# A two-layer hybrid backbone: layer 1's normalised input stored as two halves by the u projection and loaded as halves by the z projection

## The chip, the core and the metric

The kernel runs on one core of one Trainium2 chip. The time is the device time of one launch in microseconds (us). All data are 32-bit floats; a matmul operand is given as two parts, a rounded half ("hi") and the rest ("lo"), and each product is three matmuls: hi·hi, hi·lo and lo·hi.

## The reference, cut to what matters

Layer 0 is windowed attention, layer 1 a bidirectional state-space layer (S5). The change touches layer 1's input only:

```
h  = rmsnorm(x, norm_w[1]) * (1.0 + scale[:, None]) + shift[:, None]     # 2048 x 1024, called h1 here
u, z = jnp.split(h @ w_in, 2, axis=-1)                                   # w_in 1024 x 2048
...                                                                      # two scans over u, forward and backward
y  = gelu(y.reshape(b, l, SSM_WIDTH), approximate=False)
ya, yg = jnp.split(y @ w_glu, 2, axis=-1)
out = ((ya * sigmoid(yg)) * silu(z)) @ w_out
```

Both u and z are products of the same h1. The kernel computes u early and z much later, so h1 has to come a second time from somewhere.

## The kernel before, in words

Time runs through numbered phases: the attention layer (phases 1 and 2), the u projection (phase 3, about 1318 to 1520 us in the profile), the chunk states of the S5 layer (phase 4, to about 1696), the z projection with the scan over chunks (about 1696 to 1930), the S5 outputs (phase 5), and the GLU and output projection (phases 6 and 7). Tensor tiles are 128 partitions deep; "L1425" is line 1425 of the kernel.

**Order.** The code names an engine for each instruction; a scheduler that runs when the program is built sets the order of instructions on each engine, and a few instructions are pinned. Each engine works through its own row in that order. DMAs are issued from the row of SyncE ("SPq") or of ScalarE ("ACTq", through the helper `st`, L136), so a transfer whose buffer isn't free holds up all that stands behind it in the same row.

**u projection** (`phase3`, L1236). Eight blocks u of 256 tokens. `prep(u)` loads two row blocks of the layer's input x1d (L1255, tiles `qta` and `qtb` in turn, block 0 as `xt`), normalises them, and calls `prep3` (L1205) four times: TensorE transposes, ScalarE scales and shifts into an unrounded tile `hf` (named `kctx` in the profile, L1213), VectorE rounds it to `hi` (L108), VectorE or GpSimd subtracts to `lo` (L111). `st(store, hf)` then writes the unrounded tile, 256 KB, to the DRAM scratch `h1d` on ScalarE's queue: 32 such stores in all. TensorE multiplies the halves of block u while block u+1 is prepared.

**z projection** (`zproj`, L1427). The loops are nh (two halves of the 8 column blocks n) over u (8 token blocks) over np (two pairs of n): 16 passes (nh, u), called blocks i below. In each, 4 quarters q of the depth are multiplied for each n, 6 matmuls each: 96 a block, 1,536 in all. The weights of a column block n are loaded raw and split (`load_w`, tiles `wzh`, `wzl`; the low half on VectorE for n < 4, on GpSimd for n >= 4). `load_h` loads 256 KB of h1d into a raw tile `zraw` (4 buffers, shared with the weights, L1457), rounds it on ScalarE (L106), and subtracts on GpSimd (L111) into one of five tiles `zh0` to `zh4`; block 0 does some of this on VectorE. A block's four loads are asked for during the second pair of the block before. The result goes through ScalarE (`zo`, L1496, Silu) to the scratch z1d.

**The scan** (`scan`, L1405) runs on VectorE in the same stretch: 142 steps that each depend on the one before, a step being two multiplications (L1420) and four additions (L1425) with both inputs in SBUF, except the first two steps, whose products lie in PSUM (`kps`). Phase 5 (`rest`, first matmuls at L1669, their operand `xT` copied by ScalarE from the scan's result `sall`, L1662 and L1664) needs the finished scan. `first` and `early` (L1569, L1743) prepare tables for it: they are called inside the z projection's loop. Among them are L1536, L1539, L1544, L1561 and L1564 on VectorE and L1531, L1560 and L1592 on GpSimd.

Of the kernel before, what the change touches and what calls it, by code (L numbers as in the profile page):

```python
# [6 lines left out]
F32 = mybir.dt.float32  # L7
F32R = mybir.dt.float32r
# [9 lines left out]
KT = 8  # L18
# [47 lines left out]
ZH = ['vv', 'vv', 'vg', 'vv']  # L66
SZ = 2
# [18 lines left out]
class Net:  # L86
# [1118 lines left out]
    def prep3(self, k, src, t, hi, lo, r, store=None, hf=None):  # L1205
        nc = self.nc
        for kk in range(2):
            for j in range(2):
                nc.tensor.transpose(t[:, kk, j * 128:(j + 1) * 128], src(j, (k + kk) * 128), self.ident)
        if hf is None:  # L1210
            hf = self.k3()
        for kk in range(2):
            nc.scalar.activation(hf[:, kk], t[:, kk], AF.Identity, scale=self.g1[:, k + kk, r:r + 1],  # L1213
                                 bias=self.s1[:, k + kk, r:r + 1])
        self.split(hi[:, k:k + 2], lo[:, k:k + 2], hf, "v", "g" if k % 4 else "v")
        if store is not None:
            self.st(store, hf)

    def phase3_open(self):
        nc, a = self.nc, self.a  # L1220
# [15 lines left out]
    def phase3(self, uy):  # L1236
        nc, a = self.nc, self.a
        with ExitStack() as es:
# [12 lines left out]
            def prep(u):  # L1251
                if u:
                    xs = self.kp.tile([128, 2, D], F32, name=("qta", "qtb")[u % 2])
                    for j in range(2):
                        nc.sync.dma_start(xs[:, j], self.xrows(2 * u + j))  # L1255
                else:
                    xs = x0
                ss = sq.tile([128, 2], F32, name="ss3")
                for j in range(2):
                    junk = sq.tile([128, D], BF16, name="junk3", bufs=1)  # L1260
                    nc.scalar.activation(junk, xs[:, j], AF.Square, accum_out=ss[:, j:j + 1])
                r = self.rstd(sq, ss, 2)
                for j in range(2):
                    (nc.vector if u == 0 and j == 0 else nc.gpsimd).tensor_scalar(xs[:, j], xs[:, j], r[:, j:j + 1], 1.0, op0=OP.mult,
                                                                                  op1=OP.mult)
                hi = sm.tile([128, KT, 256], F32R, name="hi3")
                lo = sm.tile([128, KT, 256], F32R, name="lo3")
                for k in range(0, KT, 2):
                    self.prep3(k, lambda j, c: xs[:, j, c:c + 128], ps.tile([128, 2, 256], F32, name="tp3"), hi, lo, 0,
                               self.h1d[u][:, k:k + 2],  # L1270
                               xh.tile([128, 2, 256], F32, name=f"hf{k}") if u == 0 and k < 4 else None)
                H[u] = (hi, lo)

# [153 lines left out]
    def zproj(self, ps, first, early, scan):  # L1427
# [5 lines left out]
        pc = ec.enter_context(self.pool("zpc"))  # L1433

        def raw_tile():
            return pc.tile([128, 512], F32, name="zraw", bufs=4)

        W = {}

# [8 lines left out]
        H = {}  # L1448
        nh_ = [0]

        def load_h(u, qs, eng="g"):
            hs = H.setdefault(u, [])
            for q in qs:
                if nh == 0 and u == 0 and q == SZ:
                    next(scan)
                raw = raw_tile().rearrange("p (k c) -> p k c", k=2)
                nc.sync.dma_start(raw, self.h1d[u][:, q * 2:q * 2 + 2])  # L1457
                slot = nh_[0] % 5
                nh_[0] += 1
                h = (pc if slot == 4 else pa).tile([128, 2, 2, 256], F32R, name=f"zh{slot}")  # L1460
                self.split(h[:, 0], h[:, 1], raw, *(ZH[q] if eng == "v" else ("a", "g")))
                hs.append(h)

        if SZ < 0:
# [1 line left out]
        for nh in range(2):  # L1466
            for u in range(8):
                for np in range(2):
                    ns = [nh * 4 + np * 2, nh * 4 + np * 2 + 1]
                    if u == 0:  # L1470
                        load_w(ns[0])
                        if np == 0:
                            H.clear()
                            load_h(u, range(4), "v" if nh == 0 else "g")
                        load_w(ns[1])
                    ahead = np == 1 and u + 1 < 8
                    if ahead:
                        load_h(u + 1, (0,))
                    hs = H[u]
                    if (nh, u, np) == ZE:  # L1480
                        first()
                    if nh == 1 and u == 7:
# [5 lines left out]
                    for q in range(4):  # L1488
                        for n, p in zip(ns, pp):
                            self.mm3(p, lambda k: W[n][0][:, 2 * q + k], lambda k: W[n][1][:, 2 * q + k],  # L1490
                                     lambda k: hs[q][:, 0, k], lambda k: hs[q][:, 1, k], 2, q == 0, q == 3)
                        if ahead and q < 3:
                            load_h(u + 1, (q + 1,))
                    for n, p in zip(ns, pp):
                        z = pa.tile([128, 2, 128], F32, name="zo", bufs=2)
                        nc.scalar.activation(z.rearrange("p a b -> p (a b)"), p, AF.Silu)  # L1496
# [433 lines left out]
    def run(self, dbg=None):  # L1930
        nc, tc, a = self.nc, self.tc, self.a
        with ExitStack() as es:
# [6 lines left out]
            self.modd = [dr.tile([2, 3 * D], F32, name=f"mod{i}") for i in range(2)]  # L1939
            self.tabd = dr.tile([8, 128, 9, 128], F32, name="tabd")  # L1940
            self.a16d = dr.tile([128, 2, 64], F32, name="a16d")
            self.h1d = dr.tile([8, 128, KT, 256], F32, name="h1d")
            self.ucd = dr.tile([256, D], F32, name="ucd")
            self.z1d = dr.tile([8, 128, 16, 128], F32, name="z1d")
            self.qqd = dr.tile([64, 16, 512], F32, name="qqd")
# [77 lines left out]
```

## Time and profile before

| | us |
|---|---|
| median of three runs | 2673.79 (2672.64 to 2676.73) |
| the profiled execution | 2675.37 |
| its span, first to last instruction | 2673.5 |
| TensorE busy | 2540.4 (95%) |
| VectorE busy | 1624.3 (61%) |
| ScalarE busy | 1190.1 (45%) |
| GpSimd busy | 933.2 (35%) |

Mean granted TensorE clock over the span: 0.979 of full speed. In the views below, PE is TensorE, PEld its weight loads, DVE VectorE, ACT ScalarE, POOL GpSimd, SP SyncE. A group row ends with busy time and mean duration, then the idle time just before its instructions and what ended it; a timeline row begins with its start and its duration, and idle time before it stands in brackets. "x8" in such a row is the number of like instructions that it joins.

### The profile page before, as it was taken

How to read it: one execution, taken by the hardware profiler on the slowest of the kernel's cores; microseconds unless marked ns; L12 is line 12 of the kernel's file. 1: busy time of each engine (PE TensorE's matmuls, PEld its weight loads, DVE VectorE, ACT ScalarE, POOL GpSimd, SP SyncE). 2: the span in 40 equal slices, each digit the busy share in tenths (PEclk: the TensorE clock that was granted, in tenths of full speed). 3: DMA queues.
4: the chain of work that ended last, by engine and by line, in shares of the span. 5: the costliest groups of instructions: out<-in, count | busy, mean ns of one | idle time of the engine just before them, and what ended most of it. 6: DMA issues, size and time to landing. Idle time of an engine off the chain costs nothing. (4 is left out here: it accounts for less than half of the span.)

```text
span 2673.5 us, 43894 instructions
## 1 busy us (share of the span) xinstructions
PE 2540.4 (95%) x15973; PEld 2273.4 (85%) x15973; DVE 1624.3 (61%) x3816; ACT 1190.1 (45%) x2711; POOL 933.2 (35%) x778
## 2 busy tenths in 40 slices
PE   7999999998999999999899999899489899999998
PEld 5999989987988999998899988899467688888887
DVE  4772377537888888888531288799976431002454
ACT  3201210137777777777443178633189820001221
POOL 0321331213554455555241163355255222221221
PEclk9999999999999999999999989999789999999999
DMA  8464446477453434343363100344133332223542
GB/s 285 166 180 140 141 153 191 140 206 183 109 127 96 105 99 118 84 109 106 110 168 99 32 25 13 118 143 156 49 91 94 94 86 63 81 61 122 170 143 85
DMA packets 374330, 317.22 MB, mean 119 GB/s; under 512 B 64210, under 2 KB 327394, under 8 KB 374114
## 3 DMA queue, kind: packets, MB, share of 16 engines
q1 hardware_dynamic: 264722, 235.64, 31.8%
q10 hardware_dynamic: 109392, 78.76, 9.2%
q8 instruction: 127, 2.08, 0.3%
q14 instruction: 89, 0.73, 0.1%
HBM read 225.63 MB, written 88.70 MB: 118 GB/s over the span
## 5 line engine op out<-in xcount | busy, mean ns | idle before, releaser
L116 PE MATMUL mm<-hhl,whi 128*128 128x384 f32 x848 | 286.9, 341 | 3.6 <-DVE whi L108 2.7
L934 POOL TENSOR_SCALAR P<-P,ri 128x640 f32<-128x640 f32 (+2 forms) x272 | 208.7, 780 | 228.4 <-DVE ri L932 187.4
L117 PE MATMUL mm<-hhl,whi 128*128 128x384 f32 x848 | 286.8, 338 | 0.0
L118 PE MATMUL mm<-hhl,wlo 128*128 128x384 f32 x848 | 285.2, 337 | 0.6 <-DVE wlo L111 0.6
L953 DVE TENSOR_TENSOR pl<-pt,ph 128x512 fp32r<-128x512 f32 (+1 forms) x384 | 233.2, 607 | 32.6 <-ACT ph L952 30.0
L912 DVE CUSTOM_DVE_ANT_0 P<-S,mask,sink 128x640 f32<-128x640 f32 (+1 forms) x240 | 209.2, 872 | 55.9 <-PE S L903 50.6
L952 ACT ACTIVATE ph<-pt 128x512 fp32r<-128x512 f32 (+1 forms) x384 | 202.9, 529 | 73.2 <-PE pt L948 70.5
L948 PE MATMUL pt<-ident,P 128*128 128x128 f32 x1312 | 212.6, 274 | 13.0 <-DVE pl L953 5.2
L913 ACT ACTIVATE P<-P,nm 128x640 f32<-128x640 f32 (+1 forms) x256 | 208.1, 813 | 23.7 <-DVE nm L912 7.7
L948 PEld LDWEIGHTS pt<-ident,P 128*128 128x128 f32 x1312 | 156.6, 140 | 31.3 <-POOL P L934 10.8
L111 POOL TENSOR_TENSOR wlo<-wraw,whi 128x512 fp32r<-128x512 f32 x60 | 86.6, 1472 | 259.0 <-DVE whi L108 252.7
L116 PEld LDWEIGHTS mm<-hhl,whi 128*128 128x128 f32 x848 | 159.5, 189 | 14.3 <-issue 9.9
L117 PEld LDWEIGHTS mm<-hhl,whi 128*128 128x128 f32 x848 | 160.2, 189 | 6.5 <-issue 6.1
L118 PEld LDWEIGHTS mm<-hhl,wlo 128*128 128x128 f32 x848 | 160.0, 189 | 1.3 <-DVE wlo L111 0.9
L116 PE MATMUL zps<-zh,wzh 128*128 128x256 f32 x512 | 146.0, 287 | 5.1 <-ACT zo L1496 4.3
L117 PE MATMUL zps<-zh,wzh 128*128 128x256 f32 x512 | 146.2, 287 | 2.4 <-POOL zh L111 2.4
L1852 DVE TENSOR_TENSOR gy<-gps,gs 128x512 f32<-128x512 f32 x32 | 22.1, 691 | 207.4 <-POOL gs L1850 207.4
L118 PE MATMUL zps<-zh,wzl 128*128 128x256 f32 x512 | 145.9, 286 | 0.0
L1425 DVE TENSOR_TENSOR sall<-sall 128x64 f32<-128x64 f32 x560 | 141.6, 309 | 0.1
L1849 ACT ACTIVATE gs<-gps 128x512 f32<-128x512 f32 x32 | 19.1, 597 | 258.6 <-PE gps L118 258.6
L108 DVE CAST whi<-wraw 128x512 fp32r<-128x512 f32 (+1 forms) x80 | 53.5, 719 | 106.7 <-PE mm L117 86.7
L111 POOL TENSOR_TENSOR zh<-zraw,zh 128x512 fp32r<-128x512 f32 x61 | 81.6, 1344 | 101.6 <-ACT zh L106 78.3
(591 smaller groups left out, 7735.3 us busy)
## 6 DMA issues: line engine op xcount, KB each, us to landing
qta<-qd SPq DMA_DIRECT2D x144, 128.0 KB
qtb<-qd SPq DMA_DIRECT2D x144, 128.0 KB
wraw<-in_w_ada_dram SPq DMA_DIRECT2D x16, 1024.0 KB
zraw<-h1d SPq DMA_DIRECT2D x64, 256.0 KB
wraw<-in_attn_w_in_dram SPq DMA_DIRECT2D x12, 1024.0 KB
mq<-qqd SPq DMA_DIRECT2D x64, 192.0 KB
qd<-oh ACTq DMA_DIRECT2D x48, 192.0 KB
qd<-ol ACTq DMA_DIRECT2D x48, 192.0 KB
```

The costliest lines, as they stand in the source:

```text
L108: nc.vector.tensor_copy(hi, src)
L111: (nc.gpsimd if lo_eng == "g" else nc.vector).tensor_tensor(lo, src, hi.bitcast(F32), op=OP.subtract)
L116: nc.tensor.matmul(ps, whi(k), mhi(k), start=first and k == 0, stop=False)
L117: nc.tensor.matmul(ps, whi(k), mlo(k), start=False, stop=False)
L118: nc.tensor.matmul(ps, wlo(k), mhi(k), start=False, stop=last and k == nk - 1)
L912: nc.vector.tensor_tensor_reduce(o, sc, mk, -0.125, nsink[:, h:h + 1], OP.add, OP.min, nm)
L913: nc.scalar.activation(p, p, AF.Exp, bias=nm, scale=-1.0, accum_out=SM[i][:, e:e + 1])
L934: (nc.vector if e >= CTXV else nc.gpsimd).tensor_scalar(P[i][e], P[i][e], ri[:, e:e + 1], 1.0, op0=OP.mult, op1=OP.mult)
L948: ins = nc.tensor.transpose(t[:, c - c0], P[i][e][:, k * 128:(k + 1) * 128], self.ident)
L952: nc.scalar.activation(ph[:, c0:c1], t, AF.Copy)
L953: nc.vector.tensor_tensor(pl[:, c0:c1], t, ph[:, c0:c1].bitcast(F32), op=OP.subtract)
L1425: nc.vector.tensor_add(y[:, :, hs[h]], t[:, h, i], y[:, :, hs[h]])
```

## The change

`prep3` no longer stores the unrounded tile: it stores `hi` and `lo`, 256 KB each, from SyncE's queue, so 64 stores in place of 32 on ScalarE's. `h1d` is laid out so that the two halves of a quarter lie side by side. `load_h` loads both halves, 512 KB, straight into a `zh` tile (six of them now, `zh0` to `zh5`); nothing is rounded or subtracted any more. Blocks are numbered through both halves nh (i from 0 to 15), and block i+1 is asked for during block i: its first two quarters before the first pair, the others after the first two quarters of the second pair. `zraw` serves the weights alone and has two buffers instead of four. Line numbers behind L1217 are one higher in the kernel after, and the load of h is L1460.

```diff
         if store is not None:
-            self.st(store, hf)
+            for i, t in enumerate((hi, lo)):
+                nc.sync.dma_start(store[:, i], t[:, k:k + 2].bitcast(F32))
...
-                               self.h1d[u][:, k:k + 2],
+                               self.h1d[u, k // 2],
...
-            return pc.tile([128, 512], F32, name="zraw", bufs=4)
+            return pc.tile([128, 512], F32, name="zraw", bufs=2)
...
-        def load_h(u, qs, eng="g"):
-            hs = H.setdefault(u, [])
+        def load_h(i, qs):
+            hs = H.setdefault(i, [])
             for q in qs:
-                if nh == 0 and u == 0 and q == SZ:
+                if i == 0 and q == SZ:
                     next(scan)
-                raw = raw_tile().rearrange("p (k c) -> p k c", k=2)
-                nc.sync.dma_start(raw, self.h1d[u][:, q * 2:q * 2 + 2])
-                slot = nh_[0] % 5
+                slot = nh_[0] % 6
                 nh_[0] += 1
-                h = (pc if slot == 4 else pa).tile([128, 2, 2, 256], F32R, name=f"zh{slot}")
-                self.split(h[:, 0], h[:, 1], raw, *(ZH[q] if eng == "v" else ("a", "g")))
+                h = (pc if slot >= 4 else pa).tile([128, 2, 2, 256], F32R, name=f"zh{slot}")
+                nc.sync.dma_start(h.bitcast(F32), self.h1d[i % 8, q])
                 hs.append(h)
...
+                    i = nh * 8 + u
+                    if i == 0 and np == 0:
+                        load_h(0, range(1))
                     if u == 0:
                         load_w(ns[0])
-                        if np == 0:
-                            H.clear()
-                            load_h(u, range(4), "v" if nh == 0 else "g")
+                        if i == 0 and np == 0:
+                            load_h(0, range(1, 4))
                         load_w(ns[1])
-                    ahead = np == 1 and u + 1 < 8
-                    if ahead:
-                        load_h(u + 1, (0,))
-                    hs = H[u]
+                    if np == 0 and i < 15:
+                        load_h(i + 1, (0, 1))
+                    hs = H[i]
...
-                        if ahead and q < 3:
-                            load_h(u + 1, (q + 1,))
+                        if np == 1 and i < 15 and q < 2:
+                            load_h(i + 1, (q + 2,))
...
-            self.h1d = dr.tile([8, 128, KT, 256], F32, name="h1d")
+            self.h1d = dr.tile([8, 4, 128, 2, 2, 256], F32, name="h1d")
```

How the instructions stand in their rows, at three places. First SyncE's row where the z projection starts, before (`zraw` is a raw buffer, `in_ssm_w_in` the weights, `sall` and `tabd` belong to `first`):

```order
L1445 DMA zraw_19862<-in_ssm_w_in_dram 128x4x128
L1445 DMA zraw_19866<-in_ssm_w_in_dram 128x4x128
L1457 DMA zraw_19870<-h1d_66 128x512
L1457 DMA zraw_19875<-h1d_66 128x512
L1457 DMA zraw_20684<-h1d_66 128x512
L1457 DMA zraw_20689<-h1d_66 128x512
L1445 DMA zraw_20696<-in_ssm_w_in_dram 128x4x128
L1445 DMA zraw_20700<-in_ssm_w_in_dram 128x4x128
L1445 DMA zraw_20762<-in_ssm_w_in_dram 128x4x128
L1445 DMA zraw_20766<-in_ssm_w_in_dram 128x4x128
L1445 DMA zraw_20772<-in_ssm_w_in_dram 128x4x128
L1445 DMA zraw_20776<-in_ssm_w_in_dram 128x4x128
```

The weights of column block 0 stand first, then the four quarters of block 0 of h1, then all other weights of the first half. And after, where `zh0` to `zh5` are the halves' tiles:

```order
L1460 DMA zh0_19892<-h1d_66 128x1024
L1446 DMA zraw_19896<-in_ssm_w_in_dram 128x4x128
L1446 DMA zraw_19900<-in_ssm_w_in_dram 128x4x128
L1460 DMA zh1_19904<-h1d_66 128x1024
L1460 DMA zh2_20710<-h1d_66 128x1024
L1460 DMA zh3_20712<-h1d_66 128x1024
L1460 DMA zh4_20724<-h1d_66 128x1024
L1460 DMA zh5_20726<-h1d_66 128x1024
L1446 DMA zraw_20716<-in_ssm_w_in_dram 128x4x128
L1446 DMA zraw_20720<-in_ssm_w_in_dram 128x4x128
L1573 DMA sall_18297<-in_ssm_d_dram 16x64x1
L1571 DMA sall_18297<-tabd_64 128x7x64
```

The second block's first two loads now stand ahead of the weights of the second column block, and the weights of the third follow `first`'s two loads instead of coming straight behind the first block.

Second, VectorE's row at the same place, before (L111 with `zh` splits h1, with `wzl1`, `wzl2`, `wzl3` the weights of column blocks 1 to 3; L1420 and L1425 are the scan):

```order
L108 CAST zh3_20691<-zraw_20689 128x512
L1420 TENSOR_TENSOR kps_19847<-sall_18265,bco_80 128x128
L111 TENSOR_TENSOR zh3_20691<-zraw_20689,zh3_20691 128x512
L1425 TENSOR_TENSOR sall_18265<-kps_19847,sall_18265 128x2x32 x2
L111 TENSOR_TENSOR wzl1_20695<-zraw_20696,wzh1_20694 128x512
L1425 TENSOR_TENSOR sall_18265<-kps_19847,sall_18265 128x2x32 x2
L1420 TENSOR_TENSOR kps_19847<-sall_18265,bco_80 128x128
L111 TENSOR_TENSOR wzl1_20695<-zraw_20700,wzh1_20694 128x512
```

The scan's first step is mixed with the splits of h1 and of the weights. After (the scan is L1421 and L1426):

```order
L1421 TENSOR_TENSOR sall_18297<-sall_18297,bco_80 128x128 x2
L1426 TENSOR_TENSOR sall_18297<-sall_18297 128x2x32
L111 TENSOR_TENSOR wzl1_20715<-zraw_20716,wzh1_20714 128x512
L1552 TENSOR_TENSOR sall_18297<-ident_74,sall_18297 16x64
L1426 TENSOR_TENSOR sall_18297<-sall_18297 128x2x32 x2
L111 TENSOR_TENSOR wzl1_20715<-zraw_20720,wzh1_20714 128x512
```

The splits of h1 are gone from the row, and the low half of column block 1's weights, which stood in the scan's first step, now stands behind 39 instructions of the scan: six steps and part of the seventh.

Third, SyncE's row in the u projection, before (`xt3`, `qtb` and `qta` are the inputs of blocks 0, 1 and 2; the rest loads parameters of the S5 layer):

```order
L1245 DMA xt3_15853<-x1d_61 128x1024 x2
L397 DMA craw_16587<-in_ssm_c_re_dram 128x4x64 x2
L406 DMA raw_ssm_b_re_16590<-in_ssm_b_re_dram 64x32x16
L1255 DMA qtb_16029<-x1d_61 128x1024 x2
L1255 DMA qta_16304<-x1d_61 128x1024 x2
```

No store of h1 is in this row. After (`hi3` and `lo3` are the halves of block 0; the first four of its stores stand just above this piece):

```order
L397 DMA craw_16599<-in_ssm_c_re_dram 128x4x64 x2
L1218 DMA h1d_66<-hi3_15883 128x512
L406 DMA raw_ssm_b_re_16602<-in_ssm_b_re_dram 64x32x16
L1218 DMA h1d_66<-lo3_15884 128x512
L1218 DMA h1d_66<-hi3_15883 128x512
L1218 DMA h1d_66<-lo3_15884 128x512
L1256 DMA qtb_16033<-x1d_61 128x1024 x2
L1256 DMA qta_16312<-x1d_61 128x1024 x2
```

All eight stores of block 0's halves now stand ahead of the loads of blocks 1 and 2.

## Rows read from the trace of the kernel before

**Rows 1.** the page's section 1: busy us, share of the span, instructions

```profile
PE 2540.4 (95%) x15973; PEld 2273.4 (85%) x15973; DVE 1624.3 (61%) x3816; ACT 1190.1 (45%) x2711; POOL 933.2 (35%) x778
```

**Rows 2.** ten-us windows of all engines; columns stand in the first line

```profile
core 0: us, PE busy (x) PEld busy (x) DVE busy (x) ACT busy (x) POOL busy (x), PEclk, DMA share, GB/s
...
1730.00:1740.00 10.00, 5.94 (x42) 5.45 (x41) 9.84 (x40) 2.49 (x14) 2.58 (x3) 0.81 0.08 27
1740.00:1750.00 10.00, 8.87 (x51) 8.35 (x52) 10.00 (x37) 4.73 (x15) 5.15 (x4) 0.68 0.55 169
...
1810.00:1820.00 10.00, 10.00 (x83) 9.63 (x83) 10.00 (x19) 4.46 (x9) 8.25 (x7) 1.00 0.60 193
...
1900.00:1910.00 10.00, 0.00 (x0) 0.00 (x0) 10.00 (x65) 0.00 (x0) 0.00 (x0) 0.50 0.00 1
```

**Rows 3.** groups by line and form, 1897 to 1928 us (PE and GpSimd idle)

```profile
L1425 DVE TENSOR_TENSOR sall<-sall 128x64 f32<-128x64 f32 x132 | 20.4, 210 | 0.0
L1420 DVE TENSOR_TENSOR sall<-sall,bco 128x128 f32<-128x128 f32 x66 | 15.8, 277 | 0.0
```

**Rows 4.** the same view, 1746 to 1890 us (z projection running)

```profile
L1425 DVE TENSOR_TENSOR sall<-sall 128x64 f32<-128x64 f32 x334 | 95.1, 342 | 0.0
...
L111 POOL TENSOR_TENSOR zh<-zraw,zh 128x512 fp32r<-128x512 f32 x48 | 64.0, 1337 | 64.8 <-ACT zh L106 62.7
L1420 DVE TENSOR_TENSOR sall<-sall,bco 128x128 f32<-128x128 f32 x166 | 61.9, 411 | 0.0
...
L111 POOL TENSOR_TENSOR wzl<-zraw,wzh 128x512 fp32r<-128x512 f32 x8 | 10.3, 1318 | 1.6 <-ACT wzh L106 1.6
```

**Rows 5.** TensorE in order of time: start us, us, instruction, idle before

```profile
1896.80 0.28 PE L118 MATMUL zps<-zh,wzl 128*128 128x256 f32 x1
1929.76 3.78 PE L1669 MATMUL yp<-uy,xT 128*128 128x256 f32 x8 [32.68 <-ACT xT L1664]
```

**Rows 6.** ScalarE and VectorE in order of time around the scan's end

```profile
1936.90 0.66 ACT L1496 ACTIVATE zo<-zps 128x256 f32<-128x256 f32 x2
...
1927.90 0.61 DVE L1425 TENSOR_TENSOR sall<-sall 128x64 f32<-128x64 f32 x4
...
1940.40 1.23 DVE L1544 TENSOR_TENSOR gr<-tab 128x1024 f32<-128x1024 f32 x1 [2.69 <-DMA z1d<-zo]
```

**Rows 7.** work on the tile zps by stretch: PE, PEld, ACT, clock, DMA

```profile
1696.00:1760.00 64.00, 56.33 (x429) 54.57 (x430) 6.11 (x17) 0.92 0.48 149
1760.00:1800.00 40.00, 40.00 (x336) 40.00 (x335) 5.21 (x14) 1.00 0.44 135
1800.00:1830.00 30.00, 27.56 (x219) 26.34 (x219) 3.56 (x10) 1.00 0.62 191
1830.00:1897.00 67.00, 67.00 (x560) 66.88 (x558) 8.47 (x22) 1.00 0.42 128
```

**Rows 8.** SyncE's DMA issues where the z projection starts

```profile
1678.52 9.80 SPq L1445 DMA_DIRECT2D zraw<-in_ssm_w_in_dram  x2
1688.37 5.67 SPq L1457 DMA_DIRECT2D zraw<-h1d  x4
1694.32 5.50 SPq L1445 DMA_DIRECT2D zraw<-in_ssm_w_in_dram  x5
```

**Rows 9.** u projection: GpSimd, SyncE and ScalarE in order of time

```profile
1335.16 1.30 POOL L111 TENSOR_TENSOR lo<-kctx,hi 128x512 fp32r<-128x512 f32 x1 [3.83 <-DVE hi L108]
...
1335.56 0.82 SPq L1255 DMA_DIRECT2D qtb<-x1d  x2
...
1339.56 1.06 ACT L1261 ACTIVATE junk<-qtb 128x1024 bf16<-128x1024 f32 x1 [1.97 <-DMA qtb<-x1d]
```

**Rows 10.** windows with the DMA share and GB/s at their ends

```profile
1340.00:1360.00 20.00, 20.00 (x173) 20.00 (x172) 8.15 (x20) 10.68 (x31) 11.62 (x10) 1.00 0.79 212
...
1690.00:1720.00 30.00, 27.76 (x220) 26.75 (x221) 25.95 (x72) 19.12 (x39) 11.22 (x11) 1.00 0.67 200
1744.00:1750.00 6.00, 6.00 (x43) 6.00 (x43) 6.00 (x22) 1.68 (x4) 3.06 (x3) 0.80 0.76 233
```

## The prediction

> **What bounds the kernel now.** TensorE is busy for 95% of the span, VectorE for 61% [rows 1], so the first look is for the stretches in which TensorE isn't busy. The ten-us windows show one: from 1900 to 1920 TensorE, ScalarE, GpSimd and the DMA queues do nothing, VectorE alone is busy, and the granted clock is at 0.50, the lower of its two levels [rows 2]. In order of time the z projection's last matmul starts at 1896.80, and the next matmul at 1929.76, after 32.68 us of idling for the copy xT [rows 5]. That copy needs the scan, and the scan's last addition starts at 1927.90 [rows 6]. So in this stretch the bound is the scan on VectorE. The same 33 us hold up ScalarE: the last zo of the z projection runs at 1936.90, and VectorE's L1544 waits for its store until 1940.40 [rows 6].
>
> Why is the scan so late? The groups by line answer. With TensorE and GpSimd idle, 132 additions and 66 multiplications are 33 steps in 31.2 us, 0.945 us a step [rows 3]. While the z projection runs, 334 additions are 83.5 steps in 144 us, 1.72 a step; the same instructions take 342 ns for 210, and 411 for 277 [rows 4]. In that stretch the slow-down is 144 - 83.5 x 0.945 = 65 us, and GpSimd was busy with 64.0 us of low halves of h1, 10.3 of those of the weights [rows 4] and two tables of some 2 us each, 78 in all. That is 0.83 us of VectorE lost for each us of GpSimd. Where GpSimd is at 8.25 of 10 us VectorE gets 19 instructions done, where it is at 5.15, 37, and where it is at 0, 65 [rows 2]. I take it that GpSimd's subtractions slow the scan, and by their own length.
>
> TensorE's own work in the z projection is 1,536 matmuls. At full pace 560 take 67 us, 0.120 each [rows 7], so 184.3 us are needed and about 200.8 used (1696 to 1896.8). By stretch, 64 - 429 x 0.12 = 12.5 us are lost before 1760 and 30 - 219 x 0.12 = 3.7 between 1800 and 1830, where the weights change [rows 7].
>
> **The change part by part.**
>
> *GpSimd's 61 subtractions, ScalarE's 60 casts and VectorE's few splits of h1 go.* 142 steps at 0.945 are 134 us. VectorE still has six low halves of weights and first's tables, 13 us by estimate (a dozen operations of the kind of L1544's 1.23 [rows 6]). GpSimd keeps the weights' low halves, 10.3 us, and some tables, not more again; I take 17 us, at 0.83, so 14. With 3 for waits, the scan that begins at about 1698, two us behind the first z matmul, ends near 1863, some 30 us before TensorE's last matmul. Then it bounds nothing, and the late end is TensorE's own.
>
> *The end E of the z projection.* SyncE now puts six loads of 512 KB ahead of the second column block's weights, and VectorE puts 6.5 steps of the scan, 6 us, ahead of their low half. In the trace, raw weights whose load began at 1694.32 stood behind 1.5 MB; now they stand behind 3.5 MB [rows 8]. At 200 GB/s [rows 10] the extra 2 MB are up to 10 us, but the queue begins at 1678.52 and the first ten us of it were spent on a buffer [rows 8], so I take the weights to be there at about 1701 and their low half at 1705. Column block 0 fills 24 x 0.12 = 2.9 us of this; the rest is idle: 5 us for the second block, 3 for the third and 2 more for the fourth and the lower clock, 10 in all (6 to 20). At the change of weights only two raw buffers are left, and the weights stand behind loads of h1 in SyncE's row: 5.5 us where 3.7 were lost (2 to 12). In between, each load has the time from the release of its tile to its first matmul, at least 60 matmuls or 7.2 us, and comes from DRAM in about 4 (qtb, issued at 1335.56, was used at 1339.56 [rows 9]). So E = 1696 + 184.3 + 15.5 = 1896, the same as now within a us. The change buys nothing on TensorE itself here.
>
> *What follows E.* Phase 5's first matmul no longer waits for the scan: 1929.76 would become about E + 0.3, a gain of 33.5. ScalarE's last zo would run at E + 0.5 instead of 1936.90, and L1544 at about E + 4 instead of 1940.40, a gain of 40 [rows 6]: between the two lie phase 5's first tables, which can now be made before E by engines that would otherwise be idle. TensorE also comes in at the full level of its clock: out of the pause at 0.50 [rows 2] its first eight matmuls took 3.78 us, waits for xT among it [rows 5], where eight at full pace are 0.96. The next bound behind both is TensorE's row of phase 5, where nothing is changed. I take 41 (33.5 if only the idle time is saved, 44 with all of the slow clock).
>
> *The u projection.* TensorE is busy for all 20 us of each window here [rows 10], so anything late costs. 64 stores from SyncE replace 32 from ScalarE. The eight of block 0 stand ahead of the loads qtb and qta, and the last of them waits for a low half that ends at 1336.46 [rows 9]. qtb was issued at 1335.56; it would be issued at about 1338, 2 to 3 us later. Block 1 has little to spare, later blocks have a whole block (25 us) less their own preparation. The queues are at 0.79 and 212 GB/s here [rows 10], and the further 1 MB in 25 us is 42 GB/s: some of the cover goes. ScalarE saves 32 issues. I take +2 (0 to +6).
>
> *Sum.* 0.9 us from E, 41 less 2: about -39 of the profiled execution's 2675.4 us, 2636.4. The median of the runs is 1.6 below that execution, so 2635.
>
> DRAM traffic is the price. Block by block, 2.1 MB of halves and 0.5 MB of stores of z in 11.5 us are 227 GB/s, where the trace of this stage shows 128 to 191 [rows 7]. The best stretch shown is 233 GB/s at a share of 0.76 [rows 10], so by proportion 306 would go; I take it as enough. The Trainium skill ("SBUF — State Buffer", section "A bandwidth-pool intuition that's wrong (but worth ruling out)") says "HBM is almost always your end-to-end bottleneck", which speaks against loading twice the bytes to save engine work. With the page's 358 GB/s the stage's 46 MB (33.5 of halves, 8.4 of z, 4.2 of weights) would take 129 us, an estimate, less than its matmuls; the sum would stay. No row here shows a sustained 358.
>
> **The rivals.**
>
> *Smoother than I think.* The stalls at the start and at the change shrink, since ScalarE and GpSimd no longer stand between load and matmul: E near 1888, gain 50, 2625. If no stall at all were left E would be 1880.4 and the time 2618; that is the floor. For it speaks that a matmul's operand now has a whole block of lead where it had half of one.
>
> *Rougher start, or loads that only just keep up.* At 200 GB/s, the rate of 1690 to 1720 [rows 10], 46 MB from 1686 take until 1916; or the start's stalls run into the lower clock, as in 1730 to 1750, where 93 matmuls worth 11.2 us took 20, so 8.8 were lost [rows 2]. E near 1915, gain 20: 2653.
>
> *The scan isn't freed.* If what slows VectorE is the matmuls, ScalarE or DMA traffic, the scan ends near 1926 as now, and the u projection's 2 us remain: 2675. Against it: windows with TensorE busy and a DMA rate of 169 against 193 GB/s differ by 37 to 19 instructions with GpSimd at 5.15 to 8.25 [rows 2].
>
> *Slower: the loads come late in every block.* If a load takes longer than its 7.2 us because loads, stores of z and their issue share the queues, TensorE pauses, the clock falls, and each pause costs 8.8 us as above. Five pauses more than assumed use up the 39 us; as a rate it decides below some 185 GB/s (46 MB from 1686 to E + 39). One pause in each of 14 blocks adds 123: 2758. For it speaks that these loads have never run at 227 GB/s; against it that 7.2 us is nearly twice what a load of this size took [rows 9], and the 306 GB/s that go by proportion. The Trainium skill's sentence quoted above ("SBUF — State Buffer") is a rule for this case; its own figure doesn't bear it out here.
>
> **How the numbers follow.** Forecast 0.60, smoother 0.12, rougher 0.15, scan not freed 0.06, slower 0.07. The likeliest is 2635; the range from the floor, 2618, to just past the rougher case, 2656, leaves out the last two and small tails. A difference under 0.2%, 5.3 us, can't be told from none here. Faster 0.88 (the first three and a little of the fourth), same 0.05, slower 0.07.
>
> **What would show it.** Right: the scan's additions at 210 to 230 ns during the z projection; its last one well before TensorE's last z matmul, near 1863; no idle time over 2 us between the last z matmul and the first L1670; E near 1896; the u projection's windows full but for 2 us. Wrong: L1426 still at 340 ns without GpSimd (scan not freed); TensorE waiting for DMA into zh in many blocks and clock rows of 0.5 (slower or rougher); E under 1890 (smoother); a gap at block 1 of the u projection over 6 us.

## The result, and the profile after

| | before | after |
|---|---|---|
| median of four runs, us | 2673.22 (2670.63 to 2676.73) | 2650.76 (2644.84 to 2655.81) |
| profiled execution: its span | 2673.5 | 2653.6 |

The ratio of the runs is 0.991, with a 95% interval of 0.9888 to 0.9932. The same kernel run again, beside new runs of the one before, gave 2642.5 for 2671.73, 0.9891 (0.9865 to 0.9918). So the change takes 22 to 29 us off, where 39 were forecast; the time lies in the stated range, near the figure of the rival "rougher start".

Both kernels issue 15,973 matmuls, in the same order but for parts of the u and the z projection, and the marks below lie outside those parts. So the starts of the n-th matmul in both traces show where the time went. Worked out that way (us between marks; "again" is the second profile of the changed kernel):

| stretch | before | after | again | after - before | forecast |
|---|---|---|---|---|---|
| start of the span to n = 3,300 | 556.3 | 556.7 | 555.8 | +0.4 | 0 |
| attention, n = 3,300 to 4,000 | 117.9 | 127.7 | 125.6 | +9.8 | 0 |
| rest of attention, u projection, phase 4 | 1021.9 | 1021.7 | 1018.0 | -0.2 | +2 |
| z projection, first to last matmul | 200.7 | 205.7 | 206.2 | +5.0 | -0.9 |
| last z matmul to n = 12,800 | 73.8 | 38.4 | 38.5 | -35.4 | -41 |
| n = 12,800 to the last | 694.1 | 694.7 | 694.5 | +0.6 | 0 |

The windows after answer to [rows 2] (columns as there: busy time and instructions of TensorE, its weight loads, VectorE, ScalarE, GpSimd, then the clock, DMA share and GB/s):

```profile
1710.00:1720.00 10.00, 5.47 (x26) 5.06 (x26) 9.55 (x41) 2.29 (x5) 3.06 (x5) 0.66 0.39 91
1720.00:1730.00 10.00, 6.65 (x34) 6.66 (x35) 10.00 (x29) 2.55 (x5) 2.75 (x4) 0.66 0.32 93
...
1740.00:1750.00 10.00, 10.00 (x86) 9.66 (x85) 10.00 (x65) 1.54 (x4) 0.00 (x0) 1.00 0.76 292
...
1800.00:1810.00 10.00, 10.00 (x86) 10.00 (x85) 4.79 (x31) 2.47 (x6) 2.37 (x2) 1.00 0.67 232
1810.00:1820.00 10.00, 10.00 (x85) 9.16 (x83) 0.89 (x5) 2.42 (x5) 2.77 (x3) 1.00 0.96 335
1820.00:1830.00 10.00, 8.13 (x53) 7.66 (x52) 9.90 (x37) 3.55 (x7) 4.92 (x4) 0.83 0.42 110
...
1890.00:1900.00 10.00, 10.00 (x86) 10.00 (x85) 0.00 (x0) 1.00 (x3) 0.00 (x0) 1.00 0.66 208
...
1910.00:1920.00 10.00, 5.99 (x36) 5.17 (x35) 7.07 (x12) 4.63 (x11) 5.56 (x5) 1.00 0.34 105
```

No window is left with TensorE idle throughout; the 20 us of [rows 2] with VectorE alone at work are gone. From 1740 VectorE gets 65 instructions done in 10 us beside full matmuls, GpSimd at 0, as it did in the pause before. From 1890 to 1900 VectorE has nothing left to do: the scan is over. And 1710 to 1730 is the new weak place: 26 and 34 matmuls, clock at 0.66. A second one, 53 at 0.83, stands where the weights change.

The scan's groups by line after, 1740 to 1800 us, answer to [rows 4]:

```profile
L1426 DVE TENSOR_TENSOR sall<-sall 128x64 f32<-128x64 f32 x256 | 39.5, 211 | 0.0
...
L1421 DVE TENSOR_TENSOR sall<-sall,bco 128x128 f32<-128x128 f32 x127 | 30.5, 278 | 0.0
```

211 ns for 342, beside the z projection's matmuls and loads of halves at up to 292 GB/s. The first matmuls of phase 5 answer to [rows 5]; in order of time after:

```profile
1911.81 1.89 PE L1669 MATMUL yp<-uy,xT 128*128 128x256 f32 x8
...
1919.44 1.37 PE L1669 MATMUL yp<-uy,xT 128*128 128x256 f32 x4 [4.01 <-ACT xT L1664]
```

The first one follows the last z matmul without idle time; the 32.68 us are gone. But the last row waits 4.01 us for ScalarE's xT.

### The profile page after: what moved, and what is told of

Same layout as the page of the kernel before. It is cut to its first block, busy times and chain, and to the rows that moved or that the text cites. A ratio compares the mean times of both kernels' runs of the same rounds, so it can differ in the third digit from the quotient of the medians.

```text
span 2653.6 us, 43792 instructions
## 1 busy us (share of the span) xinstructions
PE 2540.3 (96%) x15973; PEld 2273.7 (86%) x15973; DVE 1556.6 (59%) x3809; ACT 1154.7 (44%) x2651; POOL 851.2 (32%) x717
## 5 line engine op out<-in xcount | busy, mean ns | idle before, releaser
L111 POOL TENSOR_TENSOR wlo<-wraw,whi 128x512 fp32r<-128x512 f32 x60 | 86.6, 1471 | 258.2 <-DVE whi L108 251.9
L1850 POOL TENSOR_TENSOR gs<-gs,gz 128x512 f32<-128x512 f32 x32 | 43.6, 1364 | 206.7 <-ACT gs L1849 198.9
L118 PEld LDWEIGHTS zps<-zh,wzl 128*128 128x128 f32 x512 | 100.7, 197 | 8.7 <-DVE wzl L111 7.6
```

The costliest lines, as they stand in the source:

```text
L111: (nc.gpsimd if lo_eng == "g" else nc.vector).tensor_tensor(lo, src, hi.bitcast(F32), op=OP.subtract)
L118: nc.tensor.matmul(ps, wlo(k), mhi(k), start=False, stop=last and k == nk - 1)
L1850: nc.gpsimd.tensor_tensor(sg, sg, z, op=OP.mult)
```

## The experiments

### What made the scan slow: GpSimd's subtractions put back

```diff
                 nc.sync.dma_start(h.bitcast(F32), self.h1d[i % 8, q])
+                nc.gpsimd.tensor_tensor(h[:, 1], h[:, 1].bitcast(F32), h[:, 0].bitcast(F32), op=OP.subtract)
```

> The changed kernel with 64 GpSimd subtractions of 128x512 put back: each loaded low half is overwritten by low minus high half (the product is then another one; no work is left out). Theory A, GpSimd's subtractions slow the scan, 0.83 us for each of theirs: 64 x 1.3 = 83 us of them add about 69 us, the steps go from 0.945 to about 1.65 us on average, the scan's last addition comes again behind the last z matmul by 15 to 35 us, and the time is back at 2665 to 2680. Theory B, what freed the scan were ScalarE's casts or the raw loads that are gone: steps stay near 0.945 us and the time within 5 us of the changed kernel's.

The groups by line of this kernel, 1750 to 1890 us, and its first matmul of phase 5 (lines are one higher, L1461 is the added subtraction):

```profile
L1426 DVE TENSOR_TENSOR sall<-sall 128x64 f32<-128x64 f32 x335 | 91.7, 331 | 0.0
...
L1461 POOL TENSOR_TENSOR zh<-zh 128x512 fp32r<-128x512 f32 x48 | 63.9, 1334 | 67.9 <-DMA zh<-h1d 62.4 <-PE zps L118 5.5
L1421 DVE TENSOR_TENSOR sall<-sall,bco 128x128 f32<-128x128 f32 x167 | 62.3, 411 | 0.0
```

```profile
1931.03 3.35 PE L1670 MATMUL yp<-uy,xT 128*128 128x256 f32 x7 [23.44 <-ACT xT L1665]
```

335 additions are 83.75 steps in 140 us, 1.67 a step, at 331 and 411 ns as in [rows 4]. The scan's last addition began at 1929.5, 22 us behind the last z matmul at 1907.3, and TensorE idled 23.44 us for xT. One run gave 2675.88, beside a median of 2675.38 for the kernel before. In its trace the z projection and the stretch behind it to n = 12,800 take 270.0 us, where the kernel before took 274.5 and the changed one 244.1. Theory A holds in its place, its price and its sign: ScalarE's casts and the raw loads are still gone here, and nearly the whole gain is gone all the same.

The changed kernel shows the same instruction by instruction, where GpSimd still splits weights. VectorE in order of time, and GpSimd beside it:

```profile
1818.82 0.21 DVE L1552 TENSOR_TENSOR sall<-ident,sall 16x64 f32<-16x64 f32 x1 [14.03 <-PE kps L1638]
...
1821.86 0.61 DVE L1426 TENSOR_TENSOR sall<-sall 128x64 f32<-128x64 f32 x4
...
1822.81 2.79 DVE L1426 TENSOR_TENSOR sall<-sall 128x64 f32<-128x64 f32 x4
```

```profile
1822.71 2.53 POOL L111 TENSOR_TENSOR wzl<-zraw,wzh 128x512 fp32r<-128x512 f32 x2 [4.87 <-ACT wzh L106]
```

Four additions took 0.61 us one step earlier and 2.79 here, beside GpSimd's 2.53 of two subtractions. VectorE lost 2.18 of 2.53 us, 0.86 of GpSimd's time, where the prediction had 0.83 from averages. The Trainium skill ("SBUF — State Buffer", section "Who interferes with whom") says that a VectorE instruction with two SBUF inputs contends with a GpSimd instruction that reads SBUF; these rows agree.

### Whether the attention phase's 10 us belong to the change

The changed kernel unaltered, and the kernel before with a scratch of the new size:

```diff
-            self.h1d = dr.tile([8, 128, KT, 256], F32, name="h1d")
+            self.h1d = dr.tile([8, 128, KT, 512], F32, name="h1d")[:, :, :, 0:256]
```

> The changed kernel once more, unaltered. Its profiled execution lay 9.3 us behind the kernel before at the end of a stretch of the attention phase (555 to 645 us) in which both run the same instructions in the same order. Theory A, that lag differs from execution to execution (the runs of the changed kernel lie between 2644.8 and 2655.8): another profile shows another lag there, between 0 and 10 us, and the span follows it. Theory B, the changed kernel really is later there: again about 9 us. In both, the z projection takes 205 to 206 us from first to last matmul and the first phase 5 matmul comes within 1 us of it.

> The kernel before, with its scratch h1d of the changed kernel's size (half of each row unused), so that what lies behind it in DRAM lies where it lies in the changed kernel; nothing else. Theory A, where the scratch lies doesn't matter and the lag in the attention phase is by execution: the time is that of the kernel before within 3 us. Theory B, the place of the scratch makes the attention phase slower: later by 5 to 10 us, with the lag at 555 to 645 us.

The unaltered kernel took 2642.5 (0.9891, 0.9865 to 0.9918), the padded one 2673.03 for 2671.73 (1.0004, 0.9984 to 1.0024; one of its ten executions took 12,897.5 us, and without it the median is 2671.32). The stretch from matmul 3,300 to 4,000 took 117.9 in the first profile of before and 127.7 in that of after; here 125.6 in the changed kernel, 126.5 in the padded kernel before, and between 118.1 and 125.7 in eight more kernels that share the changed u projection. So it is a difference between executions, not the change, and the place of the scratch in DRAM made none: theory A twice, though the unaltered kernel, 7.7 us behind, wouldn't have decided it alone. The profile of before happens to hold the shortest such stretch and that of after the longest, which hides 10 us of the gain in that pair. Of the 9.8 us between those two, 5.4 are idle time of TensorE (15.7 against 21.1 us in the stretch) and 4.4 longer busy time at a lower granted clock (0.97 against 0.92); the padded kernel before shows 0.92 too. Why one execution has more of both than another stays open.

### The z projection's start: buffers or order

The prediction had 10 us lost at the start; the first 240 matmuls took 43.9 us where 28.8 is the full pace (240 at 0.120), so it was 15. In order of time in the changed kernel, VectorE, SyncE and TensorE:

```profile
1713.33 0.48 DVE L1421 TENSOR_TENSOR sall<-sall,bco 128x128 f32<-128x128 f32 x2
1713.73 0.21 DVE L1426 TENSOR_TENSOR sall<-sall 128x64 f32<-128x64 f32 x1
1713.87 0.68 DVE L111 TENSOR_TENSOR wzl<-zraw,wzh 128x512 fp32r<-128x512 f32 x1
```

```profile
1700.63 1.53 SPq L1446 DMA_DIRECT2D zraw<-in_ssm_w_in_dram  x2
...
1713.87 0.37 SPq L1571 DMA_DIRECT2D sall<-tabd  x1
1714.57 14.85 SPq L1446 DMA_DIRECT2D zraw<-in_ssm_w_in_dram  x6
```

```profile
1710.72 0.38 PE L116 MATMUL zps<-zh,wzh 128*128 128x256 f32 x1 [1.57 <-ACT wzh L106]
...
1714.60 0.58 PE L118 MATMUL zps<-zh,wzl 128*128 128x256 f32 x1 [3.38 <-DVE wzl L111]
...
1723.35 0.58 PE L118 MATMUL zps<-zh,wzl 128*128 128x256 f32 x1 [3.78 <-DVE wzl L111]
```

VectorE begins the low half of column block 1's weights at 1713.87, behind six steps of the scan. TensorE waits for it until 1714.60, 3.38 us. Only then is one of the two raw buffers free, and SyncE can issue the third block's weights, from 1714.57; their low half is late in turn, and TensorE waits another 3.78 us, all with the lower clock behind it. With the 1.57 us for a high half, TensorE idles 8.7 us here; most of the other 6 us are the lower clock (49 matmuls come 0.21 us apart, where 0.12 is the full pace). In SyncE's row a load of `first` (L1571) stands just ahead of these weights and left only at 1713.87. So VectorE's order, the two buffers and that load lie in a row, and five kernels bear on them. First the low halves on GpSimd:

```diff
-                self.split(W[n][0][:, ks], W[n][1][:, ks], raw, *(ZW if n == 0 else ("a", "v" if n < 4 else "g")))
+                self.split(W[n][0][:, ks], W[n][1][:, ks], raw, *(ZW if n == 0 else ("a", "g")))
```

> The low halves of the weights of column blocks 1 to 3 on GpSimd in place of VectorE, nothing else. Theory A, at the start these low halves are late because VectorE has over six steps of the scan and first's tables ahead of them: the loss at the start falls from 14 to about 9 us, the scan is longer by some 6 x 1.3 x 0.83 = 6.5 us less the 4 us of the subtractions, which nobody waits for, and the time falls by 4 to 5. Theory B, the raw buffers' loads set the start and not VectorE's order: the loss stays at 13 to 14 and the time is the same within 2.

It went the other way: 52.0 us for the first 240 matmuls, the z projection 213.3, 2652.29 (0.9925, 0.9896 to 0.9955). In order of time in that kernel, GpSimd, SyncE and TensorE:

```profile
1701.14 2.60 POOL L111 TENSOR_TENSOR wzl<-zraw,wzh 128x512 fp32r<-128x512 f32 x2 [26.81 <-ACT wzh L106]
1709.26 5.82 POOL L1592 TENSOR_TENSOR uy<-sall 128x256 f32<-128x256 f32 x8 [5.51 <-DMA sall<-tabd]
```

```profile
1706.46 0.37 SPq L1571 DMA_DIRECT2D sall<-tabd  x1
1706.93 19.01 SPq L1446 DMA_DIRECT2D zraw<-in_ssm_w_in_dram  x6
```

```profile
1711.14 0.58 PE L116 MATMUL zps<-zh,wzh 128*128 128x256 f32 x1 [4.24 <-ACT wzh L106]
1716.35 0.58 PE L118 MATMUL zps<-zh,wzl 128*128 128x256 f32 x1 [4.42 <-POOL wzl L111]
```

The low halves of column block 1 now come early, and both raw buffers are free at 1703.74. But the next weights leave only at 1706.93, behind first's load L1571 in SyncE's row, and TensorE waits 4.24 us for their high half. Then GpSimd's row has eight products of first (L1592) ahead of their low halves, and those wait for the table that L1571 loads: 4.42 us more. Neither theory had that: the order of SyncE's row and that of GpSimd's took back more than the move gave. Next, four raw buffers, paid for with one tile of halves:

```diff
-            return pc.tile([128, 512], F32, name="zraw", bufs=2)
+            return pc.tile([128, 512], F32, name="zraw", bufs=4)
...
-                slot = nh_[0] % 6
+                slot = nh_[0] % 5
```

> Four raw buffers for the weights as before, paid for with one tile of halves (five, not six). Theory A, two raw buffers and the scan ahead of the weights' low halves cost the 14 us lost at the z projection's start and the 7 at its change of weights: the start loses about 8, the change about 4, the z projection takes about 196 us in place of 205.7, and the time falls by 8 to 10 against the changed kernel. Theory B, a load of halves needs the lead of six tiles (with five it is 5.8 us for a load of about 4): TensorE waits for DMA in several blocks, with the lower clock behind it, and the time is equal or higher by 10 or more.

The first 240 matmuls took 33.6 us (4.8 lost), the z projection 193.8, and 120 matmuls around the change of weights 15.4 in place of 20.7. The time was 2633.59 (0.9854, 0.983 to 0.9878), 9 us under the changed kernel in the same series. Theory A, with its size. Theory B's wait is there, but it is small:

```profile
PEld zps L116 <- DMA zh<-h1d: 1.8, 5, 0.6
```

The last 696 matmuls took 86.1 us for 83.4 with six tiles. So the lead of five tiles just does, and the changed kernel traded a buffer that mattered for one that hardly did. At the start, though, the edit changed more than the buffers, since the scheduler made other rows of it. VectorE in that kernel:

```profile
1702.07 0.68 DVE L111 TENSOR_TENSOR wzl<-zraw,wzh 128x512 fp32r<-128x512 f32 x1
```

This low half of column block 1 stands behind three steps of the scan and part of the fourth, where it stood behind six and part of the seventh. TensorE waits 2.37 us for it in place of 3.38. The third block's weights leave at 1692.65, long ahead of first's load L1571 (1707.41), and their low halves come ahead of first's products in VectorE's row. Third, VectorE's order with the two buffers kept:

```diff
-                if i == 0 and q == SZ:
+                if (i, q) == (1, 0):
                     next(scan)
```

> The changed kernel with the scan started one block of the program later, so that VectorE's row has the low halves of column block 1's weights ahead of the scan and those of blocks 2 and 3 in its first steps; still two raw buffers. Low halves on GpSimd made the start worse (52.0 us for the first 240 matmuls, 43 with them on VectorE), because GpSimd's row has first's eight products ahead of them. Theory A, VectorE's order delays the release of the two raw buffers by 6 us and with it all later weights: the first 240 matmuls take about 37 in place of 43 us and the time falls by 5. Theory B, the two buffers alone set the pace of the weights' loads: 42 to 43 us, the same time.

The first 240 matmuls took 33.3 us, the z projection 194.9, and the time was 2636.8 (0.9873, 0.9857 to 0.989). The windows of the changed kernel's second profile, then of this one:

```profile
1700.00:1710.00 10.00, 5.05 (x33) 4.65 (x32) 8.86 (x48) 4.00 (x7) 0.00 (x0) 0.81 0.46 114
1710.00:1720.00 10.00, 6.62 (x33) 6.42 (x32) 9.83 (x20) 2.67 (x6) 5.80 (x8) 0.68 0.34 100
```

```profile
1700.00:1710.00 10.00, 8.06 (x62) 7.44 (x62) 3.00 (x10) 6.70 (x13) 0.00 (x0) 1.00 0.64 220
1710.00:1720.00 10.00, 9.06 (x70) 8.36 (x69) 6.90 (x33) 3.07 (x6) 0.00 (x0) 1.00 0.54 135
```

33 matmuls at 0.68 became 70 at 1.00. Theory A, with 10 us where 6 were expected for the first 240: with the low halves ahead, the third and fourth blocks' weights come one after the other in time, though there are still two buffers, and the clock stays at 1.00. The scan's first addition came 5 us later, counted from the first z matmul, and its last one began at 1872.3, 25 us before the last z matmul. (The edit moves first's loads behind those of the weights in SyncE's row too; how much of the 10 us that brings wasn't separated.) The interval of the time overlaps that of the changed kernel, 0.9865 to 0.9918: that this is faster rests on the trace. At the change of weights nothing moved, 20.6 us: there four buffers help and the later scan doesn't.

Both cures of the start, and buffers with GpSimd's low halves:

> Four raw buffers, five tiles of halves, and the scan started a block later. With four raw buffers alone the first 240 matmuls took 33.6 us where 28.8 is the full pace. Theory A, what is left there is VectorE's order: 30 to 31 us, the z projection in about 191, 2630 to 2632. Theory B, it is the loads of the weights behind those of the halves: still 33 to 34, and the time of four raw buffers alone.

> Both edits together: four raw buffers with five tiles of halves, and the weights' low halves of column blocks 1 to 3 on GpSimd. If both are causes of the loss at the start: the start loses about 4 us in place of 14, the change of weights about 4 in place of 7, and the time falls by about 12 against the changed kernel, to some 2638. If only the raw buffers matter: as with four raw buffers alone, within 2 us. If five tiles are too few: TensorE waits for DMA in several blocks and nothing is gained.

Buffers and order together: 31.8 us for the first 240, the z projection 192.1, 2635.27 (0.987, 0.985 to 0.9889). That is between the two theories at the start, and in time not to be told from either alone. Either edit alone removes two thirds of the loss at the start. But both put the low halves earlier in VectorE's row and the third block's weights ahead of first's load L1571, so these kernels don't tell how much belongs to the buffers, to VectorE's order and to that load. Buffers and GpSimd's low halves: 38.5 us, the z projection 199.9, 2640.92 (0.9885, 0.9861 to 0.9908); the move to GpSimd cost 5 here as it cost 9 with two buffers. None of its three expectations is met.

The whole of the z projection's matmuls in one row each (busy us and count of TensorE, its weight loads and ScalarE for the tile zps, then clock, DMA share and GB/s of the window): the changed kernel, four buffers, the later scan.

```profile
1690.00:1960.00 270.00, 192.92 (x1536) 190.70 (x1536) 24.45 (x64) 0.94 0.59 188
```

```profile
1690.00:1960.00 270.00, 188.65 (x1536) 186.43 (x1536) 24.38 (x64) 0.97 0.62 195
```

```profile
1690.00:1960.00 270.00, 187.96 (x1536) 185.15 (x1536) 24.30 (x64) 0.98 0.61 193
```

The same 1,536 matmuls are busy for 192.92, 188.65 and 187.96 us, as the mean clock goes from 0.94 to 0.97 and 0.98: some 5 us of the start's loss were the lower clock itself, since the later scan changes the start alone.

### What holds phase 5's start

```diff
-                    if np == 0 and i < 15:
+                    if np == 0 and i < 12:
...
-                        if np == 1 and i < 15 and q < 2:
+                        if np == 1 and i < 12 and q < 2:
...
-                    hs = H[i]
+                    hs = H[min(i, 12)]
...
-                    if nh == 1 and u == 7:
+                    step = {(14, 0): 0, (15, 1): 1}.get((i, np))
+                    if step is not None:
...
```

> The changed kernel without the loads of the last three blocks of the z projection (blocks 13 to 15 multiply block 12's halves again), so that the buffers behind the halves' tiles 4 and 5 are free one block earlier and phase 5's first table is loaded a block earlier; all matmuls are done. Theory A, phase 5's start now waits for that table (landed 7.4 us before the last z matmul, and 12 us of GpSimd, VectorE and ScalarE work follow before the last zo): the last zo comes within 1 us of the last z matmul in place of 5, VectorE's L1544 about 4 us earlier, and the time falls by 3 to 5. Theory B, phase 5's start is bound by something else: the last zo and the time stay within 1 us.

In the changed kernel, GpSimd, ScalarE and VectorE in order of time:

```profile
1904.48 2.20 POOL L1531 TENSOR_TENSOR gr<-tab 128x1024 f32<-128x1024 f32 x1 [74.18 <-DMA tab<-tabd]
```

```profile
1915.61 0.84 ACT L1621 ACTIVATE g<-gi 64x256 f32<-64x256 f32 x2 [3.75 <-POOL sall L1560]
1916.47 0.38 ACT L1496 ACTIVATE zo<-zps 128x256 f32<-128x256 f32 x1
...
1917.31 0.38 ACT L1496 ACTIVATE zo<-zps 128x256 f32<-128x256 f32 x1 [0.46 <-ACT zo L1496]
```

```profile
1920.02 1.23 DVE L1544 TENSOR_TENSOR gr<-tab 128x1024 f32<-128x1024 f32 x1 [2.73 <-DMA z1d<-zo]
```

GpSimd had waited for the first table until 1904.48, 7.2 us before the last z matmul; ScalarE's L1621 waits for what follows from it, and the last two zo stand behind that in ScalarE's row: 1916.47 and 1917.31, where the last z matmul had started at 1911.7. VectorE's L1544 waits for their store. With the table earlier:

```profile
1860.86 2.21 POOL L1532 TENSOR_TENSOR gr<-tab 128x1024 f32<-128x1024 f32 x1 [38.99 <-DMA z1d<-zo]
```

```profile
1902.79 0.84 ACT L1622 ACTIVATE g<-gi 64x256 f32<-64x256 f32 x2
1903.65 0.38 ACT L1497 ACTIVATE zo<-zps 128x256 f32<-128x256 f32 x1
...
1904.49 0.38 ACT L1497 ACTIVATE zo<-zps 128x256 f32<-128x256 f32 x1 [0.46 <-PE yp L1670]
```

```profile
1907.22 1.23 DVE L1545 TENSOR_TENSOR gr<-tab 128x1024 f32<-128x1024 f32 x1 [6.58 <-DMA z1d<-zo]
```

Lines are one higher here than in the changed kernel, and the last z matmul starts at 1903.3. The table is used 42 us before it, the last zo starts 1.2 us behind it (5.6 in the changed kernel), the instruction that was L1544 3.9 behind it (8.3), and matmul 12,800 comes 34.2 us behind it (38.4). Theory A. The time, 2644.03 for 2675.38 (0.9894, 0.9871 to 0.9917), is that of the changed kernel within the interval: 4 us are less than the runs can tell here.

### A version with both

Later scan, four raw buffers, and, with nothing left out, the table a block earlier:

```diff
-                slot = nh_[0] % 5
+                slot = (1, 2, 3, 0)[nh_[0] % 4] if i > 13 else nh_[0] % 5
...
-                    if nh == 1 and u == 7:
+                    step = {(14, 1): 0, (15, 1): 1}.get((i, np))
+                    if step is not None:
...
```

> The same, and the last two blocks' halves go to the four tiles that phase 5's first table doesn't need, so that the table is loaded a block earlier, with nothing left out. Theory A, phase 5's start waited for the table (4.2 us in the kernel without the last loads): the stretch from the last z matmul to matmul 12800 falls from 38 to about 34 us and the time by 4, to some 2627. Theory B, four tiles are too few for the last two blocks: TensorE waits for DMA there, once or twice for 1 to 3 us with the lower clock behind it, and the gain is lost.

2629.95 us (0.9843, 0.9826 to 0.9859): 42 us under the kernel before, the lowest ratio of all, though its interval overlaps that of four raw buffers alone. From the last z matmul to matmul 12,800 it took 35.5 us (37.1 without the earlier table), and the z projection 192.3, as without it. Theory A by its sign, less than half of its size. The first wait for xT, without and with the earlier table:

```profile
1899.94 2.08 PE L1669 MATMUL yp<-uy,xT 128*128 128x256 f32 x4 [5.08 <-ACT xT L1664]
```

```profile
1900.77 1.13 PE L1670 MATMUL yp<-uy,xT 128*128 128x256 f32 x4 [0.77 <-ACT xT L1665]
```

The 4 us are gone at that place, but two later waits grew, to 2.71 us for xT and 2.73 for VectorE's `bm`. And the table's products now stand between the scan's steps: its last addition begins at 1892.3, only 4 us before the last z matmul, where it was 21. So a still earlier table might bring the scan back as the bound; that wasn't tried.

## Why the prediction was right, and where it was short

**The bound and its cause.** The scan on VectorE, slowed by GpSimd: shown by taking the subtractions away (342 to 211 ns) and by putting them back (331 ns, and nearly the whole gain gone). The end of the scan was forecast 165 us behind its start; it took 169.1. That is close by luck, since two errors cancel. The rest of VectorE's work cost some 21 us, less than the 27 set for it and the 3 for waits, and VectorE idled 14.03 us at 1818.82 for phase 5's small matmuls (the row above, L1552), which wait in TensorE's row behind z matmuls. The row was in the order all along and I hadn't priced it. It cost nothing, since 35 us were left.

**The first term that failed: the z projection.** Forecast 15.5 us of stalls (10 at the start, 5.5 at the change), E 0.9 us better; measured 21.4 (205.7 - 184.3): 15 at the start and 6.3 at the change. The place was right, and so was the idling: 5 us for the second column block and 3 for the third were forecast, 1.57 + 3.38 and 3.78 measured. The term that was too small is the "2 more for the fourth and the lower clock": no wait for the fourth block shows, but the lower clock and a few small matmuls of phase 5 among these 240 took the other 6 us. The bound of 6 to 20 held it. Either edit alone took the start back to some 33 us; that first's load in SyncE's row is part of the chain was not in the forecast.

**The second: phase 5's start.** Forecast 41, measured 35.4. The 32.7 us of idling went, as forecast. The step that failed is "phase 5's first tables can now be made before E". Their own load waits for buffers that the last blocks of halves hold, so they are made from 1904 to 1917 around E, and the last zo came at E + 5.6 in place of E + 0.5. The experiment with the earlier table, without the last three blocks' loads, gave 4.2 us of the missing 5.6; with nothing left out it was 1.7.

**The u projection.** Forecast +2, measured -0.2 and -3.9 in two profiles for it together with the rest of attention and phase 4, against one profile of the kernel before; against the padded kernel before (1018.9 us) the same two are +2.8 and -0.9. So the total doesn't tell. The delay was there. In order of time after, SyncE and ScalarE, to hold against [rows 9]:

```profile
1345.11 0.69 SPq L1218 DMA_DIRECT2D h1d<-lo  x1
1345.89 1.82 SPq L1256 DMA_DIRECT2D qtb<-x1d  x2
```

```profile
1352.14 1.06 ACT L1262 ACTIVATE junk<-qtb 128x1024 bf16<-128x1024 f32 x1 [1.75 <-DMA qtb<-x1d]
```

From issue to use qtb took 6.25 us where it had taken 4.0, and the trace of after lay 7.1 us behind here, so its use came 5.5 us late. By the lag of its matmuls TensorE lost 3.8 us on blocks 1 to 3 and had gained 2.4 at the phase's first transposes. But the padded kernel before, with the old u projection, shows a gain of 2.7 and a loss of 2.0 at the same places, so some 2 us of the loss are the change's.

**DRAM traffic.** 227 GB/s were needed; the windows above show 208 to 335 with TensorE full. The slower rival, loads late in every block, didn't come: no wait of a z matmul for halves with six tiles, 1.8 us in all with five, 2.6 with five and the later scan.

Between the sum, 2636.4, and the profiled 2655.8 lie then 6 us of the z projection, 5.6 of phase 5's start, 9.8 of an attention phase that varies by itself, less 2 of the u projection. (The terms of the sum, 0.9, 41 and -2, make 39.9 and not 39; nothing hangs on it.) That the first median came out near the rival "rougher start" is chance: that rival wanted E some 19 us later, and the z projection grew by 5.

## What to carry to other kernels

An engine's share of the time says little about whom it slows (GpSimd was busy for 35% here): look for an instruction whose mean duration differs between stretches, and which engine is busy in the slow one. When work is moved from engines to DMA, count what the buffers held that paid for it. Delays in one row of waits hang together, each holds up the issue of what the next needs; and then one cure of several can do. An edit of the buffers also lets the scheduler change the rows, so read them again before an effect is put down to the buffers.

## What was not expected

GpSimd and VectorE: 0.86 us of VectorE lost per us of GpSimd in a single pair of instructions, 2.79 us in place of 0.61. VectorE beside loads at 292 GB/s and full matmuls runs the same 211 ns as alone. A stretch of the attention phase, 700 matmuls with the same instructions in the same order, took between 117.9 and 127.7 us from one execution to another, half of the gain in question; the longest idled more and ran at a lower clock, and why stays open.
